# A softmax with relative position bias: first store and fourth load issued together, behind most of the third load, and 45 more waits on ScalarE

## The chip, the cores and the metric

The kernel runs on one core of one Trainium2 chip. The metric is device time in microseconds (us); the profile is one execution of the program as the hardware profiler recorded it. A core has 16 DMA engines between HBM and its on-chip memory SBUF (128 partitions), and compute engines that run side by side: here VectorE (DVE) and ScalarE (ACT) do nearly all the work, SyncE (SP) issues the loads, and GpSimd (POOL) makes two small index tables. Engines wait for each other and for transfers through semaphores; a DMA raises its semaphore by 16 when all of it has landed.

## What is computed

For logits of shape (2, 8, 2112, 2112) in fp32 and a table rel_bias of shape (8, 33):

```python
pos = np.arange(S)
rel = pos[:, None] - pos[None, :]
bias = rel_bias[:, np.clip(rel, -16, 16) + 16]
logits = logits + bias[None]
logits = logits - logits.max(axis=-1, keepdims=True)
exp = np.exp(logits)
return exp / exp.sum(axis=-1, keepdims=True)
```

So each row of 2112 numbers gets a bias that depends on the distance from the diagonal, and then a softmax. 285 MB are read and 285 MB written.

## The kernel before

The 2 × 8 × 2112 = 33792 rows are split over 128 partitions, 264 consecutive rows each (`ROWS`). A tile is `R` = 6 rows of every partition, 128 x 12672 numbers, 6336 KB, so each partition's share is one contiguous run of 49.5 KB in HBM. There are `N` = 44 tiles and `NBUF` = 4 buffers `X[0]` to `X[3]`, used in turn; all work is in place. Four tiles (24 rows) are a round (`STEP`).

For each tile:

- SP loads it (`load`, line 80); semaphore `ld[b]` rises by 16.
- VectorE waits for `ld[b]` and then, row by row, adds the bias from a strip `F` and takes the row's maximum, negated (`add`, line 187). Once in four tiles it copies a new strip out of a table `M` (`strip`, line 181).
- ScalarE takes the exponential of each row, with the row's sum (`exps`, line 196).
- VectorE, for three rows at a time (`HALF`), takes reciprocals of the sums (line 204) and scales the rows (line 208) in `scale`.
- ScalarE issues the store of the tile once six rows are scaled (`store`, line 84); `st[b]` rises by 16 when it has landed.
- SP waits for `st[b]` before it loads the tile that uses the buffer next, four tiles on.

A helper `take` (line 76) waits for a semaphore to reach n and lowers it by n again; so every wait of the loops has that one line. Each engine runs its own program: a loop over the rounds, with the first loads ahead of SP's loop. ScalarE's loop covers the first 40 tiles, and the last four follow written out, the last tile's store in two halves of three rows, whose landing (`landed`) ends the kernel. Loads go through SP's DMA queue (q1 in the profile), stores through ScalarE's (q10); within a queue order is kept, and all 16 DMA engines work on both queues.

The beginning is what the change touches. VectorE clears a table, ScalarE loads rel_bias into it (`rb` rises when it has landed), and VectorE builds `M` from it. SP issues, in this order: the load of tile 0; a small load of 15 partitions, 2560 numbers each, into buffer X[3] (`pad`, line 110, semaphore `even`); the loads of tiles 1 and 2; then it waits for `even` and issues the load of tile 3, which overwrites what the small load put there. After that SP's loop begins, with a wait for the first store's landing. The first store is issued as soon as tile 0 is scaled.

Of the kernel before, what the change touches and what calls it, by code (L numbers as in the profile page):

```python
# [11 lines left out]
ENG = mybir.EngineType  # L12
# [3 lines left out]
def kernel(  # L16
# [6 lines left out]
    nc = tc.nc  # L23
    P = 128
    B, H, S, S2 = logits.shape
# [3 lines left out]
    ROWS = B * H * S // P  # L29
    PB = S // ROWS  # L30
    assert ROWS * P == B * H * S and PB * ROWS == S and PB == H == 8
    R = 6
    NBUF = 4
    STEP = R * NBUF
    N = ROWS // R
    HALF = R // 2
# [1 line left out]
    MW = S + ROWS - 1  # L38
    FW = S + STEP - 1
    BIG = 3.0e38  # L40
    LOW, PAD = 32, 2560

    io = ctx.enter_context(tc.tile_pool(name="io", bufs=1))
    X = [io.tile([P, R * S], FP32, tag=f"X{b}", name=f"X{b}") for b in range(NBUF)]
# [9 lines left out]
    def view(t, offset, dims):  # L54

        return bass.AP(tensor=t.tensor, offset=t.offset + offset, ap=[[list(t.ap[0])[0], P]] + dims)

    def rows(t, j, n):

        return bass.AP(tensor=t.tensor, offset=t.offset + j * S, ap=[[ROWS * S, P], [1, n * S]])  # L60

    with tc.tile_critical(no_gpsimd_drain=True):  # L62
        ld = [nc.alloc_semaphore(f"ld{b}") for b in range(NBUF)]
# [5 lines left out]
        rb = nc.alloc_semaphore("rb")  # L69
        idx = nc.alloc_semaphore("idx")  # L70
        dve = nc.alloc_semaphore("dve")
        even = nc.alloc_semaphore("even")
        landed = tc.alloc_semaphore("landed")

        def take(eng, sem, n):
            eng.wait_ge(sem, n).then_inc(sem, -n)  # L76


        def load(j, b):
            nc.sync.dma_start(out=X[b][:, :], in_=rows(logits, j, R)).then_inc(ld[b], 16)  # L80

        def store(j, b, s0=0, n=R, sem=None):
            take(nc.scalar, scaled, n)
            nc.scalar.dma_start(
                out=rows(out, j + s0, n), in_=X[b][:, s0 * S : (s0 + n) * S]
            ).then_inc(sem or st[b], 16)
# [9 lines left out]
        def settle():  # L96
# [6 lines left out]
            out=bass.AP(tensor=F.tensor, offset=F.offset, ap=[[PB * list(F.ap[0])[0], P // PB], [1, H * W]]),  # L103
            in_=bass.AP(
                tensor=rel_bias.tensor, offset=rel_bias.offset, ap=[[0, P // PB], [1, H * W]]
            ),
        ).then_inc(rb, 16)
        load(0, 0)
        pad = X[NBUF - 1]
        nc.sync.dma_start(  # L110
            out=bass.AP(tensor=pad.tensor, offset=pad.offset + LOW * list(pad.ap[0])[0],
                        ap=[[4 * list(pad.ap[0])[0], 15], [1, PAD]]),
            in_=bass.AP(tensor=logits.tensor, offset=logits.offset + (LOW * ROWS + (NBUF - 1) * R) * S,
                        ap=[[4 * ROWS * S, 15], [1, PAD]]),
        ).then_inc(even, 16)
        for n in range(1, NBUF - 1):
            load(n * R, n)
        take(nc.sync, even, 16)
        load((NBUF - 1) * R, NBUF - 1)

        nc.gpsimd.iota(ip[:, 0], pattern=[[0, PB]], base=0, channel_multiplier=1).then_inc(idx, 1)
        nc.gpsimd.iota(ip[:, 2], pattern=[[1, PB]], base=0, channel_multiplier=0).then_inc(idx, 1)
# [16 lines left out]
        for m, op in ((eq, ALU.is_equal), (gt, ALU.is_gt), (le, ALU.is_le), (lt, ALU.is_lt)):  # L139
# [4 lines left out]
            out=view(F, 0, [[W, H], [1, W]]), in0=view(F, 0, [[W, H], [1, W]]),  # L144
# [8 lines left out]
                           in_=view(F, RT, [[Q, 2], [PB, Q // PB], [0, PB]])))  # L153
# [9 lines left out]
            out=view(F, 0, [[W, PB], [1, W]]), in0=view(F, SC + 2 * PB, [[1, PB], [0, W]]),  # L163
# [7 lines left out]
            out=view(M, U, [[ROWS, PB], [1, W]]), in0=view(F, 0, [[W, PB], [1, W]]),  # L171
            in1=view(F, SC + 8 * PB, [[1, PB], [0, W]]), op=ALU.add))
        then(v.tensor_copy(out=view(M, U + W, [[ROWS, PB], [1, ROWS - W]]),  # L173
                           in_=view(F, SC + 7 * PB, [[1, PB], [0, ROWS - W]])))
# [14 lines left out]
                    op0=ALU.add, op1=ALU.min, accum_out=nmax[:, r : r + 1],  # L189
                ).then_inc(added, 1)  # L190

        def exps(b):
            for r in range(b * R, (b + 1) * R):
                x = X[b][:, (r - b * R) * S : (r - b * R + 1) * S]
                take(nc.scalar, added, 1)
                nc.scalar.activation(  # L196
                    out=x, in_=x, func=EXP, scale=-1.0, bias=nmax[:, r : r + 1],
                    accum_out=tot[:, r : r + 1],
                ).then_inc(expd, 1)

        def scale(b):
            for r0 in range(b * R, (b + 1) * R, HALF):
                take(v, expd, HALF)
                v.reciprocal(out=rec[:, r0 : r0 + HALF], in_=tot[:, r0 : r0 + HALF]).then_inc(inv, 1)  # L204
                take(v, inv, 1)
                for r in range(r0, r0 + HALF):
                    x = X[b][:, (r - b * R) * S : (r - b * R + 1) * S]
                    v.tensor_scalar_mul(out=x, in0=x, scalar1=rec[:, r : r + 1]).then_inc(scaled, 1)  # L208

        v.sem_inc(dve, -done[0])  # L210
        with nc.Fori(0, ROWS - STEP + 1, STEP, engines=[ENG.DVE]) as j:  # L211
            strip(j)
            take(v, dve, 1)
            for b in range(NBUF):
                add(b)
                scale(b)
        with nc.Fori(0, ROWS - 2 * STEP + 1, STEP, engines=[ENG.Activation]) as j:
            for b in range(NBUF):
                exps(b)
                store(j + b * R, b)  # L220
        for n in range(N - NBUF, N):
            exps(n % NBUF)
            if n < N - 1:
                store(n * R, n % NBUF)
            else:
                store(n * R, n % NBUF, 0, HALF, landed)
                store(n * R, n % NBUF, HALF, R - HALF, landed)

        with nc.Fori(STEP, ROWS - STEP + 1, STEP, engines=[ENG.SP]) as j:
            for b in range(NBUF):  # L230
# [35 lines left out]
```

## Time and profile before

| | us |
|---|---|
| median of 3 runs | 1327.68 (1326.23 to 1330.9) |
| the profiled execution | 1327.58 |
| its span, first to last instruction | 1325.7 |
| VectorE busy | 977.9 |
| ScalarE busy | 574.3 |

The span is what the trace shows; the profiled execution's own time has 1.9 us more around it. Trace times count from the first instruction. In a view of windows a row has the stretch, the busy time of each engine with its number of instructions, the granted clock of TensorE (not used here), the DMA engines' busy share and GB/s; packets count where they start, so a short stretch can show a share above 1. In a view of DMA issues a row has the tensors, the issuing engine, the number, the size, and the us from issue to landing. Rows of a timeline begin with start and duration; the square bracket behind a row is the engine's idle time ahead of it and who ended it.

### The profile page before, as it was taken

What the parts mean: (1) busy time and instruction counts of PE and PEld (TensorE: products, weight loads), DVE (VectorE), ACT (ScalarE), POOL (GpSimd) and SP (SyncE); (2) the same over time, 40 slices, a digit from 0 to 9 for tenths busy, and PEclk for the clock granted to TensorE, in tenths of its full rate; (3) what the DMA queues carried; (4) which work ended last, traced back from release to release, by engine and by line L of the source; (5) the groups of instructions that cost most, each with busy time, mean ns of one, the idle gap of its engine ahead of it and who ended that gap; (6) DMA issues with size and microseconds to landing.
All of it is one profiled execution on the core that took longest, in us unless ns stands there. A gap on an engine that the chain in (4) does not pass through costs nothing. (4 is left out here: it accounts for less than half of the span.)

```text
span 1325.7 us, 2475 instructions
## 1 busy us (share of the span) xinstructions
DVE 977.9 (74%) x917; ACT 574.3 (43%) x538; POOL 0.4 (0%) x6
## 2 busy tenths in 40 slices
DVE  7998777667877787677778777766877787676774
ACT  3464333434444443334444443433444443333442
POOL 0000000000000000000000000000000000000000
DMA  9999999999999999999999999999999999999998
GB/s 409 419 425 440 437 424 434 440 436 422 437 439 436 425 436 439 428 430 439 440 424 433 440 437 424 436 440 431 428 437 440 425 431 440 439 422 436 439 436 355
DMA packets 12880, 571.14 MB, mean 431 GB/s; under 512 B 1455, under 2 KB 1471, under 8 KB 1471
## 3 DMA queue, kind: packets, MB, share of 16 engines
q1 hardware_dynamic: 6366, 285.63, 49.9%
q10 hardware_dynamic: 6512, 285.49, 49.8%
q14 instruction: 2, 0.02, 0.0%
HBM read 285.65 MB, written 285.47 MB: 431 GB/s over the span
## 5 line engine op out<-in xcount | busy, mean ns | idle before, releaser
L187 DVE CUSTOM_DVE_ANT_0 X<-X,F 128x2112 f32<-128x2112 f32 x264 | 605.2, 2355 | 307.5 <-DVEq L76 307.5
L196 ACT ACTIVATE X<-X,nmax 128x2112 f32<-128x2112 f32 x264 | 541.7, 2052 | 558.4 <-ACTq L76 538.3
L208 DVE TENSOR_SCALAR X<-X,rec 128x2112 f32<-128x2112 f32 x264 | 332.5, 1316 | 13.2
L196 ACT ACT_TABLE_LOAD x10 | 12.8, 1283 | 169.0 <-ACTq L76 169.0
L196 ACT ACTIVATION_READ_ACCUMULATOR X<-X,nmax 128x1 f32 x264 | 49.2, 186 | 0.0
L181 DVE COPY F<-M 128x2135 f32 x11 | 26.1, 2375 | 0.5 <-DVEq L210 0.5
L187 DVE DVE_READ_ACCUMULATOR2_ANT nmax<- 128x1 f32 x264 | 22.0, 83 | 0.0
L204 DVE RECIPROCAL rec<-tot 128x3 f32<-128x3 f32 x88 | 15.0, 171 | 0.0
L143 DVE TENSOR_TENSOR F<-F 128x264 f32<-128x264 f32 x1 | 0.4, 434 | 7.0 <-DMA F<-in_rel_bias_dram 7.0
L173 DVE COPY M<-F 128x1848 f32<-128x1848 f32 x1 | 2.1, 2079 | 0.0
L99 DVE MEMSET F<- 128x264 f32 x1 | 0.3, 278 | 1.1 <-SPq L62 1.1
L147 DVE TENSOR_REDUCE F<-F 128x33 f32<-128x264 f32 x1 | 0.6, 611 | 0.0
L170 DVE TENSOR_TENSOR M<-F 128x264 f32<-128x264 f32 x1 | 0.4, 442 | 0.0
L162 DVE TENSOR_TENSOR F<-F,rbS 128x264 f32<-128x264 f32 x1 | 0.4, 427 | 0.0
L140 DVE TENSOR_SCALAR F<-F 128x8 f32<-128x8 f32 x4 | 0.4, 168 | 0.0
L175 DVE COPY M<-rbS 128x247 f32<-128x247 f32 x1 | 0.4, 408 | 0.0
L150 DVE STREAM_TRANSPOSE F<-F 128x64 f32<-128x64 f32 x1 | 0.2, 245 | 0.0
L155 DVE STREAM_TRANSPOSE F<-F 128x64 f32<-128x64 f32 x1 | 0.2, 245 | 0.0
L160 DVE TENSOR_SCALAR F<-F,rbS 128x8 f32<-128x8 f32 x1 | 0.2, 231 | 0.0
L166 DVE SCALAR_TENSOR_TENSOR F<-F,rbS 128x8 f32<-128x8 f32 x1 | 0.2, 229 | 0.0
L161 DVE TENSOR_SCALAR F<-F,rbS 128x8 f32<-128x8 f32 x1 | 0.2, 225 | 0.0
L167 DVE SCALAR_TENSOR_TENSOR F<-F,rbS 128x8 f32<-128x8 f32 x1 | 0.2, 222 | 0.0
(15 smaller groups left out, 2.1 us busy)
## 6 DMA issues: line engine op xcount, KB each, us to landing
X<-in_logits_dram SPq DMA_DIRECT2D x44, 6336.0 KB, 40.9
out_dram<-X ACTq DMA_DIRECT2D x43, 6336.0 KB, 56.4
out_dram<-X ACTq DMA_DIRECT2D x2, 3168.0 KB, 15.5
X<-in_logits_dram SPq DMA_DIRECT2D x1, 150.0 KB, 17.5
F<-in_rel_bias_dram ACTq DMA_DIRECT2D x1, 16.5 KB, 8.1
```

What stands on the lines that cost most here:

```text
L140: then(v.tensor_scalar(out=m, in0=dp, scalar1=0.0, scalar2=None, op0=op))
L143: then(v.tensor_tensor(out=view(F, 0, [[W, H], [1, W]]), in0=view(F, 0, [[W, H], [1, W]]), in1=view(F, SC + 3 * PB, [[1, H], [0, W]]), op= ...
L147: then(v.tensor_reduce(out=F[:, RB : RB + W], in_=view(F, 0, [[1, W], [W, H]]), axis=mybir.AxisListType.X, op=ALU.add))
L162: then(v.tensor_tensor(out=view(F, 0, [[W, PB], [1, W]]), in0=view(F, SC + 2 * PB, [[1, PB], [0, W]]), in1=view(rbS, W - 1, [[0, PB], [-1, ...
L170: then(v.tensor_tensor(out=view(M, U, [[ROWS, PB], [1, W]]), in0=view(F, 0, [[W, PB], [1, W]]), in1=view(F, SC + 8 * PB, [[1, PB], [0, W]] ...
L173: then(v.tensor_copy(out=view(M, U + W, [[ROWS, PB], [1, ROWS - W]]), in_=view(F, SC + 7 * PB, [[1, PB], [0, ROWS - W]])))
L175: then(v.tensor_copy(out=M[:, 0:U], in_=low.to_broadcast([P, U])))
L181: v.tensor_copy(out=F[:, :], in_=M[:, bass.ds(ROWS - STEP - j, FW)]).then_inc(dve, 1)
L187: v.tensor_tensor_reduce(out=x, in0=x, in1=F[:, STEP - 1 - r : STEP - 1 - r + S], scale=-1.0, scalar=BIG, op0=ALU.add, op1=ALU.min, accum_ ...
L196: nc.scalar.activation(out=x, in_=x, func=EXP, scale=-1.0, bias=nmax[:, r : r + 1], accum_out=tot[:, r : r + 1],).then_inc(expd, 1)
L204: v.reciprocal(out=rec[:, r0 : r0 + HALF], in_=tot[:, r0 : r0 + HALF]).then_inc(inv, 1)
L208: v.tensor_scalar_mul(out=x, in0=x, scalar1=rec[:, r : r + 1]).then_inc(scaled, 1)
```

## The change

The pad load and its semaphore `even` go. SP now issues tile 0 and tile 1, and then tile 2 in two transfers: all but the last `CUT` = 1056 columns of the 12672 (semaphore `near`), and the last 1056 (`ld[2]`). It waits for `near`, raises a new semaphore `go`, and issues tile 3 in two halves of three rows: the first raises `front`, the second `ld[3]`. The transfers of a part have one run per partition, as before, but a shorter one.

ScalarE first does 45 waits for `rb`, which has landed long before its first exp is due. Then come tiles 0 to 2, written out: the exps of tile 0 and the first exp of tile 1, a wait for `go`, the store of tile 0, the other five exps of tile 1 and its store, three exps of tile 2, a wait for `front`, the other three and the store. Its loop starts with tile 3 and makes the same ten rounds; one tile follows it, with the store in halves as before. VectorE's program and SP's loop are unchanged.

```diff
-    LOW, PAD = 32, 2560
+    CUT = S // 2
...
-        even = nc.alloc_semaphore("even")
+        near = nc.alloc_semaphore("near")
+        go = nc.alloc_semaphore("go")
+        front = nc.alloc_semaphore("front")
...
-        load(0, 0)
-        pad = X[NBUF - 1]
-        nc.sync.dma_start(
-            out=bass.AP(tensor=pad.tensor, offset=pad.offset + LOW * list(pad.ap[0])[0],
-                        ap=[[4 * list(pad.ap[0])[0], 15], [1, PAD]]),
-            in_=bass.AP(tensor=logits.tensor, offset=logits.offset + (LOW * ROWS + (NBUF - 1) * R) * S,
-                        ap=[[4 * ROWS * S, 15], [1, PAD]]),
-        ).then_inc(even, 16)
-        for n in range(1, NBUF - 1):
+        def part(n, c0, c1, sem):
+            src = rows(logits, n * R, R)
+            nc.sync.dma_start(
+                out=X[n][:, c0:c1],
+                in_=bass.AP(tensor=src.tensor, offset=src.offset + c0, ap=[[ROWS * S, P], [1, c1 - c0]]),
+            ).then_inc(sem, 16)
+
+        for n in range(NBUF - 2):
             load(n * R, n)
-        take(nc.sync, even, 16)
-        load((NBUF - 1) * R, NBUF - 1)
+        part(NBUF - 2, 0, R * S - CUT, near)
+        part(NBUF - 2, R * S - CUT, R * S, ld[NBUF - 2])
+        take(nc.sync, near, 16)
+        nc.sync.sem_inc(go, 1)
+        part(NBUF - 1, 0, HALF * S, front)
+        part(NBUF - 1, HALF * S, R * S, ld[NBUF - 1])
...
-        def exps(b):
-            for r in range(b * R, (b + 1) * R):
+        def exps(b, r0=0, r1=R):
+            for r in range(b * R + r0, b * R + r1):
...
-        with nc.Fori(0, ROWS - 2 * STEP + 1, STEP, engines=[ENG.Activation]) as j:
-            for b in range(NBUF):
+        for _ in range(45):
+            nc.scalar.wait_ge(rb, 16)
+        exps(0)
+        exps(1, 0, 1)
+        take(nc.scalar, go, 1)
+        store(0, 0)
+        exps(1, 1, R)
+        store(R, 1)
+        exps(2, 0, HALF)
+        take(nc.scalar, front, 16)
+        exps(2, HALF, R)
+        store(2 * R, 2)
+        with nc.Fori(3 * R, ROWS - STEP - R + 1, STEP, engines=[ENG.Activation]) as j:
+            for n in range(NBUF):
+                b = (3 + n) % NBUF
                 exps(b)
-                store(j + b * R, b)
-        for n in range(N - NBUF, N):
-            exps(n % NBUF)
-            if n < N - 1:
-                store(n * R, n % NBUF)
-            else:
-                store(n * R, n % NBUF, 0, HALF, landed)
-                store(n * R, n % NBUF, HALF, R - HALF, landed)
+                store(j + n * R, b)
+        exps(NBUF - 1)
+        store((N - 1) * R, NBUF - 1, 0, HALF, landed)
+        store((N - 1) * R, NBUF - 1, HALF, R - HALF, landed)
```

## The prediction

> **What bounds the kernel now.** I read the page's busy lines, slices and queues first, then the stretches, then the two ends.
>
> ```profile
> span 1325.7 us, 2475 instructions
> DVE 977.9 (74%) x917; ACT 574.3 (43%) x538; POOL 0.4 (0%) x6
> DMA  9999999999999999999999999999999999999998
> q1 hardware_dynamic: 6366, 285.63, 49.9%
> q10 hardware_dynamic: 6512, 285.49, 49.8%
> q14 instruction: 2, 0.02, 0.0%
> X<-in_logits_dram SPq DMA_DIRECT2D x44, 6336.0 KB, 40.9
> out_dram<-X ACTq DMA_DIRECT2D x43, 6336.0 KB, 56.4
> ```
>
> No compute engine is full, the 16 DMA engines are, loads (q1) and stores (q10) half each. What rate is full shows in stretches with loads alone, at the start of the stores, and at the end:
>
> ```profile
> 0.96:1.98 1.02, 0.83 (x7) 0.00 (x0) 0.22 (x2) 1.00 0.00 0
> 18.10:40.10 22.00, 21.05 (x21) 13.62 (x13) 0.00 (x0) 1.00 1.00 432
> 40.10:60.10 20.00, 19.70 (x20) 12.89 (x12) 0.00 (x0) 1.00 1.00 406
> 1305.60:1319.60 14.00, 1.88 (x2) 0.00 (x0) 0.00 (x0) 1.00 1.00 433
> 1320.60:1324.60 4.00, 0.00 (x0) 0.00 (x0) 0.00 (x0) 1.00 0.13 57
> ```
>
> The last two columns are DMA share and GB/s. At 433 GB/s a tile of 6336 KB is 15.0 us of traffic (14.98); 88 tiles make 1318.3, so only some 7 us (0.5%) of the span can be saved. They are the first us without bytes, a dip as stores begin (20 us at 406 instead of 432: 1.2 us), and 4 us at the end in which 57 GB/s, two engines' share of 433, still move: a few DMA engines lag the rest.
>
> How the two queues share an engine:
>
> ```profile
> DMA packets 32, 1.62 MB, mean 434 GB/s; under 512 B 0, under 2 KB 0, under 8 KB 0
> q10 hardware_dynamic: 16, 0.81, 50.1%
> q1 hardware_dynamic: 16, 0.81, 50.1%
> ```
>
> That is 600 to 603.74 us, two packet times: each engine moves one load packet and one store packet. A tile is 128 packets (a partition's 49.5 KB each), eight per engine, 1.87 us apiece.
>
> Then the tail: issue times, microseconds to landing of the last load and of the two half stores of the last tile, and what the queues move from 1279.9 to 1300:
>
> ```profile
> 1245.58 0.33 SPq L80 DMA_DIRECT2D X<-in_logits_dram  x1
> X<-in_logits_dram SPq DMA_DIRECT2D x1, 6336.0 KB, 39.9
> 1303.57 4.35 ACTq L84 DMA_DIRECT2D out_dram<-X  x2
> out_dram<-X ACTq DMA_DIRECT2D x1, 3168.0 KB, 13.7
> out_dram<-X ACTq DMA_DIRECT2D x1, 3168.0 KB, 17.2
> q10 hardware_dynamic: 187, 8.67, 99.6%
> q1 hardware_dynamic: 4, 0.05, 0.6%
> ```
>
> The last load lands at 1285.5 (1245.58 + 39.9), though all but one data packet of it was under way by 1279.9. Adds, exps and scaling of three rows take until 1303.57, 18.1 us, and the DMA engines never run dry meanwhile: earlier stores are left. The second half is issued when the 4.35 us of that row end, less 0.34, at 1307.6, and lands at 1324.8. So 39.3 us of traffic follow the last load's landing: the last three stores, less what is already done of the first. That lead of loads over stores covers the last tile's compute, with little to spare.
>
> **The change part by part.** Rows of its neighbourhood: first load and pad with microseconds to landing, load 1's issue (2.45) and its 31.4 to landing, the fourth load's issue; then steps of the engines.
>
> ```profile
> X<-in_logits_dram SPq DMA_DIRECT2D x1, 6336.0 KB, 17.9
> X<-in_logits_dram SPq DMA_DIRECT2D x1, 150.0 KB, 17.5
> 2.45 16.86 SPq L80 DMA_DIRECT2D X<-in_logits_dram  x3
> X<-in_logits_dram SPq DMA_DIRECT2D x1, 6336.0 KB, 31.4
> 18.99 0.33 SPq L80 DMA_DIRECT2D X<-in_logits_dram  x1
> 9.47 0.43 DVE L143 TENSOR_TENSOR F<-F 128x264 f32<-128x264 f32 x1 [7.00 <-DMA F<-in_rel_bias_dram]
> 41.11 0.38 ACTq L84 DMA_DIRECT2D out_dram<-X  x1
> 45.52 2.06 ACT L196 ACTIVATE X<-X,nmax 128x2112 f32<-128x2112 f32 x1
> 72.11 2.06 ACT L196 ACTIVATE X<-X,nmax 128x2112 f32<-128x2112 f32 x1 [0.46 <-ACTq L76]
> 58.45 0.17 DVE L204 RECIPROCAL rec<-tot 128x3 f32<-128x3 f32 x1
> 62.80 0.34 ACTq L84 DMA_DIRECT2D out_dram<-X  x1
> 84.49 0.34 ACTq L84 DMA_DIRECT2D out_dram<-X  x1
> L76 ACTq EVENT_SEMAPHORE  x309: 17/17/17, 21.5 to 1307.5; - x155
> ```
>
> *The pad* (150 KB into X3, whose landing held the fourth load) goes: −0.36 us of traffic. It also levelled: it lands with the first load (1.42 + 17.5 and 0.96 + 17.9, both 18.9), one engine having no part of it, so without it that engine is about 0.4 us behind.
>
> *The barrier.* SP issues the third load as a main piece and a rest of 1056 columns, 0.54 MB or 1.25 us. When the main piece has landed (load 1 at 2.45 + 31.4 = 33.9, plus 11616/12672 of 15.0: 47.6), SP raises `go` and issues the fourth load in halves; ScalarE issues store 0. (Two issues more on SP, 0.33 us each as at 18.99; SP does nothing else then, and the one behind the wait is the second half, needed last.) From seeing a landing to the next issue took 0.1 us (18.9 to 18.99). The price of starting on empty queues is bounded by 1.0 (no byte from 0.96 to 1.98) and 2.9 us (first load: 17.9 for 15.0, with slow first packets and receipt). The rest covers 1.25 of it, and 0.4 is the wait for the slowest engine: between 0 and 2.2, I take 1.3, between the two since part of the 2.9 is receipt that other traffic hides. The dip of 1.2 at 40 to 60 us belongs to stores cutting into running loads; if a common start replaces it, it is saved, if it comes back, not. Pad, barrier, dip: −0.36 + 1.3 − 1.2 = **−0.3 us**, bounds −1.6 and +1.8.
>
> *The 45 waits* and those of `go` and `front` are semaphore instructions of 17 ns: 0.8 us between the bias row (used at 9.47) and the first exp at 21.5. Hidden; without that cover 0.8 us of ScalarE, which idles 57%.
>
> *What queues behind `go`.* Store 0 goes from 41.1 to about 47.8, and tile 1's second exp from 45.5 to 48.2. Its five exps, 2.06 each by that row, end at 58.5; VectorE's second reciprocal waits for them at 58.45, so store 1 moves by 0.1 to 0.3 us from 62.8. The queue needs it only when store 0 is done, beyond 70; store 2 (84.49) is needed beyond 90. `front` holds the fourth exp of tile 2, which now starts at 72.1; the half lands by about 72. Both 0.
>
> *The new lead.* This is the term that counts. From 48.9 both queues start together, but the fourth load now consists of packets of half the size (three of six rows, 24.75 KB, 0.94 us), against whole store packets of 1.87. If the engines alternate packet by packet, as with equal sizes above, store 0 (8 × 1.87) passes beside the first half load (8 × 0.94): both done at 48.9 + 22.5 = 71.4; store 1, issued at 63, passes beside the second half, done at 93.9. Load 3 then lands with store 1 instead of with store 0 or shortly after. Sizes being equal again, the lock-step lasts: load n lands with store n−2. Store n is issued 22.2 us after its load (41.11 − 18.9), the queue needs it after 30, so it never runs dry and never shifts back.
>
> By bytes instead of packets, both would take half of the rate and the lead would stay. Equal sizes can't tell the two apart; I take packets, since each engine's turn was exactly one packet. (The Trainium skill, "DMA: Bandwidth & Descriptors", section "Queues, rings and completion order", has each engine go round its queues and switch only at whole packets; by that the sum is the one below, by bytes the first rival. The trace agrees on turns; the 9 to 17 descriptors that the page gives a packet can't be seen here.)
>
> So when the last load lands, two stores are left, 30.0 us, not 39.3: it lands 9.3 later, at 1294.8. Store 42 occupies the engines until 1309.8. The last tile's first half can't be issued before 1294.8 + 18.1 = 1312.9. The engines idle, start again (1.0 to 2.9; I take 2.4, nearer the whole row, because nothing covers it) and move 15.0: landing at 1330.3, against 1324.8. **+5.5 us**, bounds +4.1 and +6.0.
>
> *Lagging engines.* The common start levels the engines at 48 us; I credit the 0.4 known at 18.9, **−0.4**, with bounds 0 and −3.5 (all but 0.5 of the 4 us at the end, were the engines to stay level).
>
> **Sum:** −0.3 + 5.5 − 0.4 = +4.8. The profiled execution took 1327.58 (span 1325.7 and 1.9 around it; the median of the runs is 1327.68): **1332.4 us**.
>
> **The rivals.** Less than 0.3% (4 us: below 1323.7 or above 1331.7) can't be told from no change.
>
> *Covered tail, level engines (faster).* Place: the hole before the last store. It vanishes if the engines share by bytes, or if the lead otherwise keeps at least 18.1 + 15.0 + 1.0 = 34.1 us of stores behind the last load; it is 39.3 now. If the levelled engines then stay together, −0.3 − 3.5 gives 1323.8; with the best barrier (−1.6) 1322.5. For: most of the engines end together at 1320.6 now, so a few laggards alone set the end. Against: something made these lag after a nearly level 18.9.
>
> *Covered tail, lag returns (no change).* −0.3 − 0.4: 1326.9. For: 88 tiles at full rate are the same traffic.
>
> *Code fetch (slower still).* ScalarE's program grows by 45 waits and a written-out prologue. Only two instruction packets, 0.02 MB, appear now. If the shifted loop needed 8 KB again in each of its ten rounds, at 27 GB/s (433/16) one engine would lose 0.3 us a round: 3 us of lag, 1335.4.
>
> That the change does nothing I rule out: store 0 could go at 41.1, and `go` can't come before about 47.
>
> **How the numbers follow.** Forecast 0.60 (1329 to 1335 within its bounds), faster rival 0.19, no change 0.13, fetch 0.08. Slower by over 0.3%: four fifths of the forecast and all of fetch, 0.56; faster: 0.16, most of the first rival; the rest 0.28. Cases of both signs hold most of the chance, so the range runs from 1323.0 to 1336.0.
>
> **What would show it.** The issue rows: loads should land after about 60 us instead of 40.9 and full stores after about 38 instead of 56.4 (8 + 30). If these stay near 41 and 56, the queues share by bytes and the forecast falls. In the tail: GB/s near 0 for some 4 us before the last store's bytes, last load landing near 1295, its first half store about 18 us later. At 46 to 51 us: one dip, then an even rate. After the last bytes: how long single engines run on; under 1 us would mean levelled engines. More than two instruction packets would speak for fetch. The forecast is wrong if the hole is there but ScalarE's issue comes sooner, or if it isn't there at all.

## The result, and the profile after

The changed kernel takes 1340.28 us (median of 19 runs), the kernel before 1327.68 us in the same rounds: a ratio of 1.0084, 95% interval 1.0069 to 1.0099. The forecast was 1332.4 us with a range from 1323 to 1336: the direction was right, the size was not. Single runs spread from 1331.89 to 1347.85 us, and of the kernel before from 1326.03 to 1339.58. The profiled execution has a span of 1339.4 us, against 1325.7.

The page of the changed kernel: span, the GB/s of 40 slices, the three queues, and the issues with their us to landing; the last line is the GB/s of the kernel before.

```profile
span 1339.4 us, 2492 instructions
GB/s 410 390 436 434 431 430 428 434 427 431 428 436 436 431 430 424 431 434 434 433 430 421 436 436 413 434 436 436 422 425 436 434 434 415 434 436 431 428 431 309
q1 hardware_dynamic: 6624, 285.48, 50.0%
q10 hardware_dynamic: 6512, 285.49, 49.3%
q14 instruction: 3, 0.02, 0.0%
out_dram<-X ACTq DMA_DIRECT2D x43, 6336.0 KB, 41.8
X<-in_logits_dram SPq DMA_DIRECT2D x42, 6336.0 KB, 56.5
...
GB/s 409 419 425 440 437 424 434 440 436 422 437 439 436 425 436 439 428 430 439 440 424 433 440 437 424 436 440 431 428 437 440 425 431 440 439 422 436 439 436 355
```

Loads and stores have changed places: 56.5 and 41.8 us to landing, where it was 40.9 and 56.4. That much was forecast. What wasn't shows faintly in the two GB/s lines: from the fourth slice to the last but two (the 38th) the changed kernel has 413 to 436, the kernel before 422 to 440, on the mean 431 against 434.

A DMA view of two stretches tells how much is lost where. First the kernel before, from 40 to 100 us and from 100 to 1270 us; under the second the two queues, with packets, MB and share of the 16 engines:

```profile
DMA packets 558, 25.77 MB, mean 429 GB/s; under 512 B 48, under 2 KB 48, under 8 KB 48
...
DMA packets 11257, 507.34 MB, mean 434 GB/s; under 512 B 1248, under 2 KB 1248, under 8 KB 1248
q10 hardware_dynamic: 5629, 253.70, 50.1%
q1 hardware_dynamic: 5628, 253.65, 50.1%
```

The same view of the changed kernel:

```profile
DMA packets 829, 24.43 MB, mean 407 GB/s; under 512 B 96, under 2 KB 96, under 8 KB 224
...
DMA packets 11169, 503.89 MB, mean 431 GB/s; under 512 B 1228, under 2 KB 1228, under 8 KB 1228
q1 hardware_dynamic: 5584, 251.62, 50.4%
q10 hardware_dynamic: 5585, 252.28, 49.8%
```

At 434 GB/s the 1.34 MB missing around the start are 3.1 us, and the 3.45 MB missing from 100 to 1270 us are 7.9 us. In that long stretch the engines are full in both kernels (the shares add up to 100%), so it is not idle time: packets take longer. Before, both queues need the same share for the same MB. After, loads need more time (50.4%) for fewer MB: 1.5% more per byte than stores, 1.90 us instead of 1.87 for a packet on the mean.

Then the tail of the changed kernel: the stretches (DMA share and GB/s are the last two columns), the issues of the last load, of the store before the last tile's (store 42), and of the last tile's two halves, with us to landing (of the halves, that of the second); at the end, store 42 of the kernel before.

```profile
1313.00:1323.00 10.00, 9.70 (x12) 6.69 (x8) 0.00 (x0) 1.00 0.29 122
1333.00:1337.60 4.60, 0.00 (x0) 0.00 (x0) 0.00 (x0) 1.00 1.03 441
...
1247.24 0.33 SPq L82 DMA_DIRECT2D X<-in_logits_dram  x1
X<-in_logits_dram SPq DMA_DIRECT2D x1, 6336.0 KB, 56.6
1296.18 0.34 ACTq L86 DMA_DIRECT2D out_dram<-X  x1
out_dram<-X ACTq DMA_DIRECT2D x1, 6336.0 KB, 24.5
1321.93 4.36 ACTq L86 DMA_DIRECT2D out_dram<-X  x2
out_dram<-X ACTq DMA_DIRECT2D x1, 3168.0 KB, 12.5
...
1277.67 0.34 ACTq L84 DMA_DIRECT2D out_dram<-X  x1
out_dram<-X ACTq DMA_DIRECT2D x1, 6336.0 KB, 32.1
```

The last load lands at 1303.9 (before 1285.5, forecast 1294.8). The first half store follows 18.05 us later, as forecast. Store 42 lands at 1320.7, the end at 1325.95 + 12.5 = 1338.4. The hole is there: from 1313 to 1323 the engines move 122 of 434 GB/s, so they idle 7.2 of 10 us on the mean. But the slowest engine ends store 42 only at 1320.7, and from there to the end are 17.7 us, where before 15.0 lay between the same two landings (1277.67 + 32.14 = 1309.81 in its trace, and 1324.80). So the hole costs 2.7 us, if the last store would else have followed store 42 as it did before. The rest of the loss, 10.9 us, had come about by the time the slowest engine ended store 42: 3.1 and 7.9 from above, less the 0.4 of the pad, which leaves 0.3 for engines that differ. **10.9 and 2.7 make the 13.6 us by which the last landing moved.**

### The profile page after: what moved, and what is told of

The parts are those of the page before. It is cut to its first block, busy times and chain, and to the rows that moved or that the text cites. A ratio compares the mean times of both kernels' runs of the same rounds, so it can differ in the third digit from the quotient of the medians.

```text
span 1339.4 us, 2492 instructions
## 1 busy us (share of the span) xinstructions
DVE 978.0 (73%) x917; ACT 567.4 (42%) x529; POOL 0.4 (0%) x6
## 5 line engine op out<-in xcount | busy, mean ns | idle before, releaser
L213 DVE TENSOR_SCALAR X<-X,rec 128x2112 f32<-128x2112 f32 x264 | 332.5, 1316 | 13.2
## 6 DMA issues: line engine op xcount, KB each, us to landing
out_dram<-X ACTq DMA_DIRECT2D x43, 6336.0 KB, 41.8
X<-in_logits_dram SPq DMA_DIRECT2D x42, 6336.0 KB, 56.5
```

## The experiments

At the outset stood these theories: that the short lead of loads over stores costs it all, by the hole at the end and by whatever else it does; that the start does, where both queues run empty and begin together; and that ScalarE's 45 waits do. Each kernel below is the changed one with one edit; the ratio is to the kernel before in the same rounds, with its 95% interval.

**The fourth load whole**, barrier and waits kept:

```diff
-        part(NBUF - 1, 0, HALF * S, front)
-        part(NBUF - 1, HALF * S, R * S, ld[NBUF - 1])
+        load((NBUF - 1) * R, NBUF - 1)
...
-        exps(2, 0, HALF)
-        take(nc.scalar, front, 16)
-        exps(2, HALF, R)
+        exps(2)
```

> The changed kernel with the fourth load whole again (no front wait); common start, go and the 45 waits stay. Two things of the changed kernel are to be told apart: a hole in the DMA traffic ahead of the last tile's store, and some 9 us more until the last load lands, in which load packets are slower on many DMA engines. Theory 1, the short lead makes both: loads and stores now finish their tiles together, and each load is issued while a whole one is still queued. Then this run has no hole (three stores follow the last load), loads land after some 31 to 41 us, and its time is that of before, 1324 to 1330. Theory 2, the common start makes the slow packets: no hole, but the stretch from 100 to 1270 us stays slow, about 1333 to 1336. Theory 3, ScalarE's waits or its shifted program make them: as theory 2.

1336.97 us, 1.0072 (1.0037 to 1.0108): most of the loss stays. Whether a part of it goes with the halves can't be told: the interval takes in the 1.0084 of the changed kernel. Of the theories, the first has the steady part right and the second the time, and none has both. This kernel's us to landing and two stretches, 60 to 100 us and 1311 to 1316 us; the last row is the kernel before:

```profile
X<-in_logits_dram SPq DMA_DIRECT2D x43, 6336.0 KB, 44.6
out_dram<-X ACTq DMA_DIRECT2D x43, 6336.0 KB, 53.1
...
60.00:100.00 40.00, 38.25 (x36) 23.61 (x22) 0.00 (x0) 1.00 1.00 386
1311.00:1316.00 5.00, 4.85 (x6) 3.87 (x4) 0.00 (x0) 1.00 0.24 101
...
60.00:100.00 40.00, 37.81 (x36) 23.63 (x23) 0.00 (x0) 1.00 1.02 441
```

The lead of loads over stores is nearly that of before (15.1 us against 18.7, by the table below), and from 100 to 1270 us the kernel moves 507.09 MB, nearly as much as before. Here the loss lies early: after the common start the engines are full (share 1.00), and yet move 386 GB/s, where the kernel before has 441 in that stretch: 5 us of work. And it lies at the end: 24% of the engines' time is busy while store 42 runs to its end.

**No barrier**: the third load whole, the halves at once behind it, store 0 as soon as it is scaled.

```diff
-        for n in range(NBUF - 2):
+        for n in range(NBUF - 1):
             load(n * R, n)
-        part(NBUF - 2, 0, R * S - CUT, near)
-        part(NBUF - 2, R * S - CUT, R * S, ld[NBUF - 2])
-        take(nc.sync, near, 16)
-        nc.sync.sem_inc(go, 1)
...
-        exps(1, 0, 1)
-        take(nc.scalar, go, 1)
         store(0, 0)
-        exps(1, 1, R)
+        exps(1)
```

> The changed kernel without the barrier: tile 2 is loaded whole, near and go are gone, store 0 is issued as soon as it is scaled; the fourth load keeps its halves, ScalarE its 45 waits. Theory 1 (the short lead makes hole and slow packets): the lead is as short or shorter by a packet or two, so hole and slowness stay, 1338 to 1345. Theory 2 (the common start makes the slow packets): only the hole stays, 1331 to 1335. Theory 3 (ScalarE's program): 1338 to 1345 as with theory 1.

1499.51 us, 1.1292 (1.1265 to 1.1318). No theory had that. The GB/s of its 40 slices, and one load and one store with their us to landing:

```profile
GB/s 414 412 436 427 425 423 423 413 383 374 387 389 386 376 374 391 371 390 390 372 389 389 372 391 370 374 389 372 389 390 375 389 385 381 393 359 390 390 238 230
...
605.77 0.33 SPq L80 DMA_DIRECT2D X<-in_logits_dram  x1
X<-in_logits_dram SPq DMA_DIRECT2D x1, 6336.0 KB, 67.5
627.55 0.34 ACTq L84 DMA_DIRECT2D out_dram<-X  x1
out_dram<-X ACTq DMA_DIRECT2D x1, 6336.0 KB, 46.0
```

The start is good (412 in the second slice, 390 in the changed kernel). But the load issued at 605.77 lands at 673.3, and the store issued at 627.55 at 673.5: load n lands together with store n−2. That is the state which the prediction took for harmless. For eight slices of 37 us, some 300 us, it moves 412 GB/s and more; then it falls to some 380: two tiles, 12.98 MB, in some 34 us instead of 29.9. From 100 to 1270 us the two queues keep the engines busy for 47.6% and 47.0% of the time: a part of the loss is idle engines, the rest packets that take longer. A buffer's round fits: 67.5 for the load, 22.2 from its landing to the store's issue, 46 for the store, 135.7 us for four tiles. But the kernel before gives the same sum with full engines (40.9 + 22.2 + 56.4 = 119.5, four times 29.9), so that sum doesn't show what sets the pace.

**Without the 45 waits:**

```diff
-        for _ in range(45):
-            nc.scalar.wait_ge(rb, 16)
```

> The changed kernel without the 45 waits, all else as in it. Theories 1 and 2: the same within 2 us, 1338 to 1342, since 45 waits of 17 ns end before the first exp is due. Theory 3 (they shift ScalarE's program so that it is fetched or runs differently, and that slows the load packets): 1330 to 1334. If the waits were a help that hides code fetches, slower, with more than three instruction packets in the trace.

1341.49 us, 1.0081 (1.0057 to 1.0105), the same as with them within the interval: the waits cost nothing that shows.

**Halves in half of the partitions**: the fourth load in three transfers, partitions 0 to 63 as two halves, the rest whole.

```diff
-        part(NBUF - 1, 0, HALF * S, front)
-        part(NBUF - 1, HALF * S, R * S, ld[NBUF - 1])
+        piece(NBUF - 1, 0, P // 2, 0, HALF * S, front)
+        piece(NBUF - 1, 0, P // 2, HALF * S, R * S, front)
+        piece(NBUF - 1, P // 2, P, 0, R * S, ld[NBUF - 1])
...
-        take(nc.scalar, front, 16)
+        take(nc.scalar, front, 32)
```

> The changed kernel with only half of the partitions (0 to 63) of the fourth load in two halves, the other 64 whole, so the stores gain four packets per engine on the loads instead of eight half ones worth four tiles' halves: 12 turns for the load against 16. The lead lies midway: 20 store packets per engine, 37 us, should follow the last load instead of 30, so by the arithmetic of the tail (18 us of compute, 15 of the last store, 1 to 3 of restart) the hole is gone or under 1 us. Theory 1 in its first form (a hole and slow packets both from loads and stores ending tiles together): slow packets fall too, 1325 to 1331. If slow packets depend on the number of loads queued rather than on the ends falling together, they stay in part: 1330 to 1336.

1340.03 us, 1.0083 (1.006 to 1.0107), as slow as the changed kernel, but the loss is elsewhere:

```profile
DMA packets 682, 20.68 MB, mean 345 GB/s; under 512 B 87, under 2 KB 87, under 8 KB 215
...
DMA packets 11270, 507.59 MB, mean 434 GB/s; under 512 B 1256, under 2 KB 1256, under 8 KB 1256
```

Loads take 52.3 us to landing and stores 45.3, between the two others: the lead is 7.5 us, four packets of 1.87, as packet by packet sharing has it for half the partitions. From 100 to 1270 us (the last line) the rate is that of before; from 40 to 100 us it lost 5.09 MB, 11.7 us. So this lead does no harm to the steady part, and the start can cost far more than it does in the changed kernel.

**Start, lead and waits taken apart further.** Four kernels: (1) neither barrier nor halves, all four loads whole and at once, no pad; (2) the same, but store 0 alone waits for the main piece of the third load (`go`); (3) the halves of half the partitions without the barrier; (4) the whole fourth load behind the main piece, store 0 as soon as it is scaled.

In outline:

```diff
 (1)    for n in range(NBUF): load(n * R, n)      # no near, go, front
 (2)    load((NBUF - 1) * R, NBUF - 1)            # ahead of take(nc.sync, near, 16)
        take(nc.sync, near, 16)
        nc.sync.sem_inc(go, 1)
 (3)    for n in range(NBUF - 1): load(n * R, n)  # then the three pieces; no near, no go
 (4)    take(nc.sync, near, 16)
        load((NBUF - 1) * R, NBUF - 1)            # no go
```

> The changed kernel without its barrier and without the halves: all four loads whole and issued at once, no pad, store 0 when it is scaled; ScalarE keeps the 45 waits and the written-out first tiles. Theory 4, formed on the first four runs: what slows is the drained common start, after which the 16 engines run both queues in step, and some of them lose 8 to 12 us to slow packets, while the halves shorten the lead and open the hole at the end. Then this run is the kernel before without its pad: 1325 to 1330, and the lead as before (loads some 41 us, stores some 56). Rival: the pad was what kept the engines together, or ScalarE's new program costs: 1333 or more.

> The changed kernel with the fourth load whole and issued at once, so that the loads never drain; only the first store waits for go (47.8 instead of 41.1 us). Theory 4: no drain, so stores cut into running loads as before; the lead is a little longer than before (loads 37 to 42 us): 1325 to 1331. Rival: holding the first store until three loads are in is itself what costs: 1333 to 1340.

> The midway lead of the run with half of the partitions in halves, but without the barrier: nothing drains, store 0 goes when scaled. Theory 4: the steady part is at 434 GB/s and the early loss of that run (367 and 339 GB/s in two slices) is gone: 1327 to 1333 with a hole of 0 to 3 us at the end. Lead theory: the lead of the halves without a barrier ended in a store queue that ran dry, at 1499; midway it is nearer to that than the changed kernel is, so 1338 or more.

> The fourth load (whole) waits for the main piece of the third, as in the change, but store 0 is issued as soon as it is scaled (41.1 us), so the store queue is already running when the loads drain and start again. Theory 4 (both queues starting together on drained engines): engines are not idle and not in step, 1326 to 1332. Rival: it is the load queue's drain that matters, whatever the stores do: 1334 to 1340 as with the whole fourth load behind the barrier (1337).

Measured: (1) 1331.74 us, 1.0025 (1.0004 to 1.0045); (2) 1331.29, 1.0027 (1.0008 to 1.0046); (3) 1541.79, 1.1597 (1.1548 to 1.1647); (4) 1520.49, 1.1481 (1.143 to 1.1532). My theory for (3) and (4), no loss where the queues don't drain and start together, was wrong by some 200 us in both. The rival for (4), 1334 to 1340, was far too low as well; that for (3), 1338 or more, had the direction only. Us to landing of loads and stores in (3), and its two queues from 100 to 1270 us:

```profile
X<-in_logits_dram SPq DMA_DIRECT2D x43, 6336.0 KB, 69.8
out_dram<-X ACTq DMA_DIRECT2D x43, 6336.0 KB, 48.1
...
q1 hardware_dynamic: 4838, 218.01, 50.0%
q10 hardware_dynamic: 4826, 217.40, 49.1%
```

In (4) it is 68.4 and 46.8. So in these two, as in the kernel without the barrier, load n lands together with store n−2, and all three lose over 150 us. In (3) the engines are nearly full (99.1%) and yet move 372 GB/s, so there it is almost wholly the packets that take longer. In (4) the fourth load is whole: there store 0 runs alone while that load waits, which shortens the lead just as well. So the loss goes with the lead, not with the way it came about. Holding only the store, (2) against (1), costs nothing that shows. Letting the fourth load wait as well, which empties both queues, costs 5.7 us more by the medians (1336.97 against 1331.29); by the two ratios and their intervals it is 1 to 11 us.

**Three more, on terms of the sum.** Loads issued later: SP waits, besides the store's landing, for a semaphore that VectorE raises after the fourth row's add. The last tile stored in 1, 2 and 3 rows instead of two halves. And the transfers of before, pad and all, with the changed kernel's ScalarE program.

```diff
+                if r == b * R + 3:
+                    v.sem_inc(late, 1)
...
+        take(nc.sync, late, 2)
...
                 take(nc.sync, st[b], 16)
+                take(nc.sync, late, 1)
                 load(j + b * R, b)
```

```diff
-        store((N - 1) * R, NBUF - 1, 0, HALF, landed)
+        store((N - 1) * R, NBUF - 1, 0, 1, landed)
+        store((N - 1) * R, NBUF - 1, 1, 2, landed)
```

> The changed kernel, but from tile 4 on each load is issued only when VectorE has also added four rows of the tile two before it, some 6 us later than the store's landing lets it go; seven load packets per engine are queued then, so the queue can't run dry. The slow load packets of the changed kernel (8 us per engine in all) lie in the 8 us after each load issue, and the store of the same buffer lands in the same place. Theory 5: the issue of a load onto a queue that holds a whole tile already slows the packets under way; then they fall to under 2 us in all and the time to 1329 to 1334 (the hole stays). Rival 5b: it is the place where the queues change tiles, or the lag among engines, whatever is issued there: slow packets stay at 6 to 9 us, 1337 to 1343.

> The changed kernel with the last tile stored as one row, two rows and three rows instead of three and three. The first piece can go some 2.5 us earlier after the last load's landing (15.5 instead of 18.1). If the hole on the slowest engine (it ends store 42 at 1320.7, the first half goes at 1321.9 and starts a us later) is worth what the trace says, the time falls by 2 to 3 us; if the hole costs the 5.5 us that I forecast, still only by 2.5, as far as the earlier issue reaches, with a hole left; if lagging engines set the end whatever the hole does, by under 1 us.

> The kernel before in all its transfers, with the pad, but with ScalarE's program of the change (45 waits, first tiles written out, loop from tile 3). Told against the run without pad and barrier (1331.7): if the pad is what it lacked, this is the kernel before, 1326 to 1329; if ScalarE's new program costs 3 to 5 us by itself, 1330 to 1333.

The first failed as an experiment: 1340.99 us, 1.0085 (1.0062 to 1.0108), but loads still took 56.4 us to landing and were issued 0.3 us after a landing, so nothing was late. The increment, an instruction of its own, did not wait for the add ahead of it: in the trace one stands at 610.87, 0.4 us after its tile's first add began (610.44), while the fourth add ends at 619.6. The second: 1336.93, 1.0055 (1.0027 to 1.0083). The median is 3.4 us better than that of the changed kernel, but the intervals overlap (three of its ten runs took some 1329 us, the others 1336 to 1343). In its profile the end comes 15.4 us after the landing of store 42 instead of 17.7, so 2.3 of the hole's 2.7 us are gone there; its span, 1338.9, is only 0.5 us shorter. The third: 1327.91, 0.9998 (0.9986 to 1.001). ScalarE's new program costs nothing, and against (1), which differs from it by the pad and the fourth load's wait for it, these are worth 3.8 us by the medians; by the two ratios and their intervals it is 0.4 to 7 us, and three of the nine runs of (1) took no longer than 1327.4.

**Late loads again**, with a semaphore that is raised by a tiny write of VectorE behind the add:

```diff
-                    v.sem_inc(late, 1)
+                    v.memset(tick[:, :], 0.0).then_inc(late, 1)
```

> The changed kernel, but SP issues each load of its loop only after the fourth row's add of the tile being worked on at that time, which is signalled by a tiny write of VectorE that stands behind that add. So the load comes some 4 to 6 us after the landing of the store that frees its buffer, instead of 0.3 us. Theory A: the load packets of the changed kernel are slow (8 us per engine over the whole run) because each load is put on a queue that still holds nearly a whole tile. Then the queue is shorter when the load comes, loads land after 51 to 53 us instead of 56.5, the slow packets fall under 3 us, the stretch from 100 to 1270 us goes back to 434 GB/s, and the time is 1330 to 1335. Theory B: they are slow because loads and stores of nearly the same age end within 3 us of each other, so that engines that have drifted change tiles against each other. The delay leaves that as it is: slow packets stay at 6 to 10 us, 431 GB/s, and the time is 1337 to 1343. If the queue runs dry because of the delay, the time goes above 1345 and the run tells neither.

1341.92 us, 1.0113 (1.0096 to 1.013). Now the load comes 6.7 us after the landing, and lands as much sooner after its issue:

```profile
X<-in_logits_dram SPq DMA_DIRECT2D x42, 6336.0 KB, 50.7
...
DMA packets 11179, 504.30 MB, mean 431 GB/s; under 512 B 1230, under 2 KB 1230, under 8 KB 1230
```

The slow load packets stay: 3.04 MB are missing from 100 to 1270 us, 3.45 in the changed kernel. Theory A falls: it isn't the issue onto a full queue. In the trace the slow packets still lie around the landings, from some 3 us before a store's landing to some 6 us behind it, and so mostly ahead of the issue now.

**The lead alone.** What was left to tell apart: the lead, or the start, which might leave the engines spread. Both kernels keep the changed start whole, barrier and halves, and give the lead back afterwards, by issuing store 2 later, so that loads run alone for some us: behind the fourth exp of tile 3 in one, behind the second in the other. Everything else is the same work; the ScalarE loop then starts with tile 4.

```diff
         exps(2, HALF, R)
+        exps(3, 0, 4)
         store(2 * R, 2)
+        exps(3, 4, R)
+        store(3 * R, 3)
```

> The changed kernel with its whole start, but store 2 is issued only behind the fourth exp of tile 3, at about 107 us instead of 85, some 8 us after store 1 has landed, so that loads run alone for those 8 us. Theory B (what costs is loads and stores ending nearly together for the rest of the run): the loads win back their lead and land 15 to 20 us ahead of store n-2 instead of 3; loads take about 40 us to landing and stores about 57, slow load packets fall under 2 us per engine, 434 GB/s or more from 130 to 1270 us, no hole before the last store. What is left is the start (+1.8 us) and engines that have drifted (0 to 4): 1328 to 1333. Rival (the start with halves spreads the engines, and that alone makes the load packets slow, whatever the lead): lead and hole as under theory B, but slow packets stay at 5 us or more, 431 GB/s, 1335 to 1341.

> The same, but store 2 goes behind the second exp of tile 3, at about 102 us: loads run alone for some 3 us. Theory B: loads land about 9 to 11 us ahead of store n-2, as near to the 7.7 us of the kernel with half of the partitions in halves as to the 15 with the fourth load whole; slow packets under 2 us, 434 GB/s, the hole shrinks to nothing or 1 us, 1328 to 1334. Rival as above: slow packets 5 us or more, 1336 to 1342.

1338.2 us, 1.0061 (1.0031 to 1.0091), and 1332.83 us, 1.004 (1.001 to 1.007). The first kernel's us to landing, MB from 100 to 1270 us, and two stretches near its end:

```profile
out_dram<-X ACTq DMA_DIRECT2D x43, 6336.0 KB, 60.0
X<-in_logits_dram SPq DMA_DIRECT2D x42, 6336.0 KB, 37.2
...
DMA packets 11241, 506.69 MB, mean 433 GB/s; under 512 B 1244, under 2 KB 1244, under 8 KB 1244
...
1307.00:1312.00 5.00, 4.85 (x6) 3.23 (x4) 0.00 (x0) 1.00 0.17 71
1328.50:1334.50 6.00, 0.00 (x0) 0.00 (x0) 0.00 (x0) 1.00 0.06 25
```

The second kernel's:

```profile
out_dram<-X ACTq DMA_DIRECT2D x43, 6336.0 KB, 49.0
X<-in_logits_dram SPq DMA_DIRECT2D x42, 6336.0 KB, 48.2
...
DMA packets 11244, 507.25 MB, mean 434 GB/s; under 512 B 1236, under 2 KB 1236, under 8 KB 1236
```

With the start unchanged, the steady part is back at 507.25 and 506.69 MB, 0.2 and 1.5 us short of before instead of 7.9. So the loss of the steady part hangs on the lead, and the rival falls. The time of the second is where theory B had it. That of the first isn't, and lies where the rival had it, so only the MB tell the two apart there: in the profiled execution a single engine (0.06 of 16, 25 of 434 GB/s) ran some 7 us longer than all others at the end. Before that the others had idled (71 GB/s from 1307 to 1312); that the late engine had held up the landings that the last tile waits for is my reading of it. That would account for the excess: 1338.0 less 7 is 1331. Of its ten runs two took 1328.9 and 1329.8, the other eight 1337.9 to 1339.5, which a single late engine, in some executions and not in others, would explain; only one of them has a trace.

The kernels side by side. "Ahead" is by how much load n lands before store n−2, the median over tiles 4 to 42; a landing is the issue plus the us to landing.

| kernel | ahead, us | MB, 100 to 1270 us | MB, 40 to 100 us |
|---|---|---|---|
| first of the last two | 22.4 | 506.69 | 24.78 |
| (1) neither | 22.1 | 506.83 | 25.92 |
| (2) store held | 21.6 | 506.89 | 25.59 |
| transfers of before, new ScalarE program | 20.3 | 506.12 | 25.92 |
| before | 18.7 | 507.34 | 25.77 |
| fourth load whole | 15.1 | 507.09 | 22.61 |
| second of the last two | 11.4 | 507.25 | 24.58 |
| halves in half the partitions | 7.5 | 507.59 | 20.68 |
| changed kernel | 3.7 | 503.89 | 24.43 |
| late loads, first try (not late) | 3.7 | 504.00 | 24.53 |
| late loads | 3.7 | 504.30 | 24.38 |
| one row first | 3.7 | 503.59 | 24.53 |
| without the 45 waits | 3.7 | 504.00 | 24.58 |
| no barrier | 0.2 | 455.13 | 25.87 |
| (4) load held | 0.2 | 449.35 | 23.98 |
| (3) halves of half, no barrier | 0.2 | 435.41 | 23.13 |

Each kernel has one trace. Two kernels with the same transfers differ by 1.2 MB in the long stretch (507.34 and 506.12), so a difference of that size means nothing. Down to 7.5 us, four packets of 1.87, no loss stands out; at 3.7 us, two packets, some 3.4 MB are missing in all five; at nothing, a tenth or more. The small leads hold: in the changed kernel it is 3.5 to 3.8 us at every tile from 4 to 42. None of these kernels is faster than the one before. The rows at 3.7 us share the halves and the common start, but so do the two kernels at 11.4 and 22.4 us.

## Why the prediction missed

**How the queues share: right.** By packets, not by bytes: 56.5 and 41.8 us to landing, 60 and 38 forecast. (The Trainium skill, "DMA: Bandwidth & Descriptors", section "Queues, rings and completion order", has each engine go round its queues at whole packets; the swap of the two numbers is what that rule gives.) The small difference matters. The first half load landed at 72.4 us and store 0 at 75.1, where both were forecast at 71.4. From 46 to 52 us the changed kernel shows, in the view of the DMA queues:

```profile
DMA packets 192, 1.35 MB, mean 225 GB/s; under 512 B 32, under 2 KB 32, under 8 KB 160
q1 hardware_dynamic: 192, 1.35, 80.0%
```

There is no row for stores: though store 0 was issued beside the first half load, each engine first took half load packets: the 32 of these (192 packets less the 160 under 8 KB) are two per engine. Two turns ahead are two store packets left over when the fourth load is done, 3.74 us. So loads stayed 3.7 us ahead, instead of level as forecast. Level is what the kernel without the barrier has, at 1499.51 us: the two turns that the barrier's start happens to give are what the changed kernel has ahead of that state, and its time is the nearer to the forecast for it. That is luck.

**The step that failed:** "Sizes being equal again, the lock-step lasts: load n lands with store n−2 … so it never runs dry and never shifts back", and with it the steady part at nothing in the sum. It never shifts back, indeed, but it isn't free. With loads ending 3.7 us ahead of the stores, load packets take longer around each change of tile: **+7.9 us**. A stretch of the changed kernel between landings (620 to 624 us) and one behind two landings (614.5 to 617 us; a load landed at 608.2, a store at 612.0), packets, MB and share:

```profile
q1 hardware_dynamic: 16, 0.81, 46.8%
q10 hardware_dynamic: 16, 0.81, 46.8%
...
q1 hardware_dynamic: 14, 0.71, 74.9%
q10 hardware_dynamic: 10, 0.51, 46.8%
```

In the first, 16 packets of each queue take 46.8% of 16 engines and 4 us: 1.87 us each. In the second, 14 load packets take 74.9% of 40 us, 2.14 each, while 10 store packets take 46.8%, still 1.87. The last two experiments show that the lead sets this, since with the same start and a longer lead it is gone; the late loads show that the moment of the issue doesn't. What makes a load packet longer when loads and stores change tiles close to each other, and whether in the DMA engines or in memory, wasn't found. Nor was it found why the level state costs far more, and in two of its three kernels only after some 300 us.

**Pad, barrier and dip: mis-sized.** Forecast −0.3 with an upper bound of +1.8; measured 3.1 − 0.4 = +2.7. The changed kernel from 40 to 60 us:

```profile
40.00:60.00 20.00, 18.82 (x19) 12.45 (x12) 0.00 (x0) 1.00 0.88 344
```

Against 434 GB/s that is 4.1 us short, 2.9 of them from 46 to 52 us (225 GB/s, the row above). Before, the dip in that stretch (406 GB/s) was worth 1.3. So the common start did take the place of the dip, but starting drained queues cost some 4 us where I took 1.3, though the rest of 1056 columns was meant to cover a part; my own bounds for it (1.0 and 2.9, less 1.25, plus 0.4) give 0.15 and 2.05, not 0 and 2.2.

**The hole: there, as forecast, at half the price.** +5.5 forecast, +2.7 measured. The 18.05 us of compute came as worked out. What was left out: the engines don't arrive together. The hole, 7.2 us of idle time per engine on the mean, swallows the lag of the slowest, since all wait for the same issue; after it they run at the full rate to the end (441 GB/s from 1333.0 to 1337.6), where before the last 4 us moved 57. So hole and lag may not be added as two terms. Storing one row first took 2.3 us off it in the trace; that it brought as much in time isn't shown.

**45 waits, `go`, `front`, code fetch: right at nothing.** The kernel without the waits runs at 1341.49, the new ScalarE program with the old transfers at 1327.91. There were three instruction packets instead of two, which was to speak for fetch; the kernel without the waits has two and is no faster.

**The rivals.** "Covered tail" fell with the lead. Engines that end level are seen, but it is the hole that levels them.

Sum by the trace: +2.7 (start), +7.9 (steady part), +0.3 (engines that differ), +2.7 (hole), 13.6 us, against +4.8. That the direction was right is in part luck, since more than half of the loss comes from the term put at nothing. By medians of neighbouring kernels the way there reads: pad taken away +3.8, store 0 held −0.4, fourth load held too +5.7, cut in halves +3.3. That these add up to 12.4, nearly the 12.6 measured, confirms nothing, since each step begins where the one ahead of it ends. By their intervals each is uncertain by 3 to 5 us; store 0 and the halves aren't clear of noise. That order of steps is one of several: the halves are worth some +3 behind the barrier, and more than +160 without it. The two parts of the change are not additive, and neither alone makes the kernel faster.

## What to carry to other kernels

When loads and stores share the DMA engines, work out by how many packets one queue ends its tile ahead of the other, and keep it at several packets: here four cost nothing in the steady part, two cost 0.6%, none 13 to 16%. A start of a few us can set that lead for the whole run: here equal packets in lock-step never gave it back. And count the MB of a long stretch against the kernel before: engines that are 100% busy in both can still be moving less.

## What was not expected of the hardware

- Load packets of 49.5 KB took 2.14 us instead of 1.87 in a stretch behind a change of tile, with store packets beside them unaffected, where both queues changed tiles within 3.7 us of each other.
- Without any lead the traffic fell to some 370 to 390 GB/s and stayed there; in two of the three kernels only after some 300 us at 401 GB/s and more.
- Fully busy engines can be slow together: behind the common start with a whole fourth load they moved 386 GB/s for 40 us, 345 with the halves in half of the partitions (from 40 to 100 us).
- A load of 150 KB at the beginning, with the fourth load waiting for it, is worth 3.8 us by the medians (1327.91 with it, 1331.74 without), 0.4 to 7 by the intervals. Why isn't shown.
- An increment of a semaphore that VectorE does as an instruction of its own wasn't held by the arithmetic ahead of it (610.87, with that add ending at 619.6).
